# Late products in another order of units, the last quarter's in one PSUM bank, and a reordered program

## The chip, the cores and the metric

The kernel runs on one core of one Trainium2 chip. The metric is the time of one execution in microseconds (us). The core has five engines that work beside one another, each through its own queue of instructions: TensorE (PE in the rows; PEld is its loading of weights), VectorE (DVE), ScalarE (ACT), GpSimd (POOL) and SyncE (SP), which here only issues transfers. Rows with a "q" behind the engine are transfers that this engine issues; an engine's queue is worked off in order.

## The reference

One layer of a backbone over 1024 latent and 256 context tokens of width 1024: an S5 mixer (a scan over the tokens in both directions, with a complex diagonal matrix, in 64 groups of 16 channels and 64 states), GELU and a gated linear layer (GLU), then a SwiGLU feed-forward layer. Both are preceded by a norm with shift and scale and followed by a gate, all made from a conditioning vector.

```python
def run(u, h0):
    bu = jnp.einsum('lgh,gnh->lgn', u.astype(F32), b_bar)
    bu = bu.at[0].add(lam_bar * h0)
    a = jnp.broadcast_to(lam_bar, bu.shape)
    _, h = lax.associative_scan(_linear_combine, (a, bu), axis=0)
    return jnp.einsum('lgn,ghn->lgh', h, c_mat).real, h[-1]
...
def out(y, h):
    y = y.reshape(h.shape).astype(h.dtype) + d_skip * h
    g = jax.nn.gelu(y)
    return g * jax.nn.sigmoid(g @ w_glu + b_glu)
```

## The kernel before, in words

The 1024 latent tokens are cut into blocks of T = 8, so there are 128 of them and the scan only goes over the states at block ends. Within a block the output is a product with small Toeplitz matrices made from the powers of the diagonal; from the states it is a product with CL, which is C times powers. Everything is held for 64 groups, worked in four quarters q of 16 groups, or in eight k of 8 groups, or in sixteen units u of 4 groups (u = 2k, 2k + 1).

VectorE runs `scan()`: 32 steps of two blocks, then 63 single ones, one dependent on the next. States in between, which no later step needs, are filled in: those of q = 0 and q = 2 by VectorE itself, as extra operations put between the dependent ones (`one()`), those of q = 1 and q = 3 by GpSimd (`fill`).

Meanwhile the other engines work through a program, a string of letters with numbers that `run` turns into instructions in that order; each engine gets its own part of it:

- A n: conditioning products on TensorE up to tile n of 64 (`ada`, line 424), each from a 256 KB load on SyncE (line 417). The loads use a ring of eight buffers; the load of tile i + 8 is written down just ahead of product i.
- C q part: a fourth of CL of quarter q (`cl_gen`), two multiplications of 128x1024 by GpSimd and then their sum. HOW says by what: PE is two blocks of four products with the identity matrix on TensorE and copies on ScalarE, SY an adding DMA that GpSimd issues (line 549).
- K: Toeplitz values of a half quarter (`k_mats`): four products per round on TensorE (lines 619 to 627), a copy on ScalarE and a write to DRAM (kd) from ScalarE's queue. K0 and K1 belong to q = 0, K2 and K3 to q = 1, and so on.
- T u: reads unit u's matrix back from kd in Toeplitz form, on SyncE (`toeplitz`, line 639), into one of four buffers KQ, so T4 to T7 overwrite what the products of units 0 to 3 read.
- L, G: loads and signs C of a quarter; M: columns of the conditioning (`mod_cols`); B: copies of B; F: a fill on GpSimd.
- R k: "restacks" the states of k for the products, eight copies on ScalarE. P k: the products of the two units of k on TensorE (`inner_mm`, lines 745 and 750), which read KQ, the input U and the restacked states. Y u: copies unit u's sum from PSUM to Y on ScalarE.
- Z i: restacks the states of the other half of the block pairs (`late_restack`), on ScalarE, VectorE and GpSimd.

After the program comes the late loop, over i = 0 to 9, in the order `order = (6, 7, 4, 5, 0, 1, 2, 3)` of k: `late_mm` multiplies the late states with CL into PSUM (line 824); `late_add` adds that to Y on VectorE, a pair of operations per k; `late_act` takes GELU of Y on ScalarE; `gt_hi` and `gt_lo` transpose on TensorE (line 841) and split for the GLU. `restack` itself is lines 727 to 729. Two w_glu blocks and b_glu are loaded by SyncE ahead of the loop (lines 890, 893), into buffers that U and the conditioning held.

All waits are set by which buffer or PSUM bank an instruction reads or writes; the order on an engine is that of the program.

Of the kernel before, what the change touches and what calls it, by code (L numbers as in the profile page):

```python
# [37 lines left out]
def s5_ffn_kernel(tc, a, out):  # L38
# [3 lines left out]
    with ctx:  # L42
# [600 lines left out]
        def fill_ops(q, d, j):  # L643
            gs = slice(8 * q, 8 * q + 8)
            o = rot_ops(ST[:, 32 + 8 * j:39 + 8 * j:2, :, d, gs], ST[:, 31 + 8 * j:38 + 8 * j:2, :, d, gs], LQ[0],
                        32 * d + 8 * q, V, sf)
            return [o[0], o[2], o[1], o[3]]

        def scan():
# [14 lines left out]
            for k in range(32):  # L664
                step(LQ[1], 31 + 2 * k, 33 + 2 * k)
                if k % 4 == 3:
                    for d in range(2):
                        rest.extend(fill_ops(0, d, k // 4))
            for j in range(8):
                for d in range(2):  # L670
                    rest.extend(fill_ops(2, d, j))
# [5 lines left out]
        def fill(q, h, reg, kb):  # L677

            tmps = [view(reg, kb + i, [256]) for i in range(2)]
            gs, c0 = slice(8 * q, 8 * q + 8), 32 * h  # L680
            for d in range(2):
                rot(ST[:, 32 + c0:63 + c0:2, :, d, gs], ST[:, 31 + c0:62 + c0:2, :, d, gs], LS[:, 0], 32 * d + 8 * q, E, tmps)

        def mod_cols(part):
            r8 = view(RC[2], 0, [4, P])
# [52 lines left out]
        def inner_mm(k, hs):  # L738

            us = (2 * k, 2 * k + 1)  # L740
            for u in us:
                inner[u] = pw([4, T, HC])
# [3 lines left out]
            for u in us:  # L746
                for i in range(4):
                    for d in range(2):
                        cs_ = slice(64 * d, 64 * d + 64)
                        PE.matmul(flat(inner[u][cs_, i]), hs_of(hs, 4 * (u % 2) + i, cs_), flat(CL[u // 4][:, d, 4 * (u % 4) + i]),  # L750
                                  start=False, stop=i == 3)

        scan()
# [4 lines left out]
        HSl = [hstate(RXc, 0), hstate(RXc, 4), hstate(RA, 8), hstate(RA, 0)]  # L758
        order = (6, 7, 4, 5, 0, 1, 2, 3)
# [6 lines left out]
        def run(prog):  # L766


            for w in prog.split():
# [19 lines left out]
                elif op == "F":  # L789
                    fill(*divmod(i, 10), *((RA, 12) if i < 20 else (RXc, 4)))  # L790
# [6 lines left out]
                elif op == "P":  # L797
                    inner_mm(i, hse[i])
                elif op == "Y":
                    S.copy(yview(i), inner[i])  # L800

        HOW = ((PE,) * 4,) + ((SY,) * 4,) * 2 + ((SY, SY, PE, PE),)
        run("A24 A28 A32 C00 A36 C01 A40 A44 C02 A48 C03 K0 K1 L2 T0 T1 T2 T3 A52 A56 C10 C11 C12 C13 A60 A64 F10 F11 R0 P0 M0 M1 Y0 Y1"
            " G2 K2 K3 L3 R1 P1 T4 T5 T6 T7 Y2 Y3 B3 B2 M2 C20 C21 G3 R2 P2 R3 Y4 Y5 P3 Y6 Y7 C22 C23 K4 K5 T8 T9 T10 T11"
            " C30 C31 C32 R4 P4 Y8 Y9 C33 K6 K7 R5 P5 Y10 Y11 T12 T13 T14 T15 F30 F31 R6 P6 R7 Y12 Y13 P7 Z1 Z0 Y14 Y15")
# [9 lines left out]
        def late_mm(i):  # L815
            hs, ps_ = HSl[i % 4], []
            for n in range(2):
                u = 2 * order[i] + n
                po = pe8([4, T, HC])
                ps_.append(po)  # L820
                for j in range(4):
                    for d in range(2):
                        cs_ = slice(64 * (1 - d), 128 - 64 * d)
                        PE.matmul(flat(po[cs_, j]), hs_of(hs, 4 * n + j, cs_), flat(CL[u // 4][:, d, 4 * (u % 4) + j]),
                                  start=True, stop=True)
# [580 lines left out]
```

## Time and profile before

| | |
|---|---|
| median of three runs | 1128.93 us (1127.88 to 1129.6) |
| profiled execution, own time | 1129.6 us |
| its span | 1127.8 us |
| its mean granted TensorE clock | 0.952 |
| TensorE busy | 1003.2 us, 89% |
| VectorE busy | 819.8 us, 73% |
| GpSimd busy | 648.8 us, 58% |
| ScalarE busy | 415.9 us, 37% |

The span is one recorded execution, from its first to its last instruction; the own time of that execution is 1.8 us longer. The granted clock is a share of TensorE's full speed of 2.4 GHz; 0.50 is 1.2 GHz. The stretch that the change touches lies between some 130 us and 317 us; the GLU and the feed-forward layer follow. The rows that matter are shown further down.

### The profile page before, as it was taken

What the parts mean: (1) busy time and instruction counts of PE and PEld (TensorE: products, weight loads), DVE (VectorE), ACT (ScalarE), POOL (GpSimd) and SP (SyncE); (2) the same over time, 40 slices, a digit from 0 to 9 for tenths busy, and PEclk for the clock granted to TensorE, in tenths of its full rate; (3) what the DMA queues carried; (4) which work ended last, traced back from release to release, by engine and by line L of the source; (5) the groups of instructions that cost most, each with busy time, mean ns of one, the idle gap of its engine ahead of it and who ended that gap; (6) DMA issues with size and microseconds to landing.
All of it is one profiled execution on the core that took longest, in us unless ns stands there. A gap on an engine that the chain in (4) does not pass through costs nothing. (4 is left out here: it accounts for less than half of the span.)

```text
span 1127.8 us, 16572 instructions
## 1 busy us (share of the span) xinstructions
PE 1003.2 (89%) x6096; PEld 804.0 (71%) x6096; DVE 819.8 (73%) x1689; ACT 415.9 (37%) x873; POOL 648.8 (58%) x502
## 2 busy tenths in 40 slices
PE   4789791677978999889999999999999999999997
PEld 1268420455878997667888888888888888888875
DVE  8889899950667797998666666666666666666657
ACT  3378521425843455222222222222222222222236
POOL 4479968665274244866655555555555555555563
PEclk9699996878998999898999999999999999999999
DMA  9876778462422201101111111111111111111104
GB/s 351 316 157 122 221 242 196 111 135 65 125 87 76 76 1 58 56 19 57 56 42 36 38 55 57 57 57 56 56 56 57 56 57 56 57 56 56 48 29 149
DMA packets 51313, 103.12 MB, mean 91 GB/s; under 512 B 4256, under 2 KB 24992, under 8 KB 49184
## 3 DMA queue, kind: packets, MB, share of 16 engines
q1 hardware_dynamic: 43456, 85.67, 22.9%
q0 software_dynamic: 3456, 12.58, 6.1%
q10 hardware_dynamic: 4320, 3.81, 1.1%
q8 instruction: 48, 0.79, 0.3%
q14 instruction: 33, 0.27, 0.1%
HBM read 83.30 MB, written 6.16 MB: 79 GB/s over the span
## 5 line engine op out<-in xcount | busy, mean ns | idle before, releaser
L70 POOL TENSOR_TENSOR c<-rxc,c 128x512 fp32r<-128x512 f32 x128 | 169.8, 1342 | 186.4 <-ACT c L1060 183.1
L70 DVE TENSOR_TENSOR ru<-pd,ru 128x512 f32<-128x512 f32 x336 | 227.0, 690 | 2.4 <-PE pd L1116 2.3
L1116 PE MATMUL pu<-ra,c 128*128 128x512 f32 x432 | 168.6, 390 | 1.3 <-POOL c L70 1.2
L1115 PE MATMUL pu<-ra,c 128*128 128x512 f32 x432 | 168.2, 389 | 0.6 <-DVE ra L70 0.6
L1114 PE MATMUL pu<-ra,c 128*128 128x512 f32 x432 | 168.4, 390 | 0.3 <-ACT ra L1060 0.3
L1060 ACT CAST c<-rxc 128x512 fp32r<-128x512 f32 x128 | 76.7, 616 | 187.2 <-POOL rxc L70 107.2
L1114 PE MATMUL pd<-c 128*128 128x512 f32 x336 | 133.3, 397 | 10.9 <-DVE ru L70 10.9
L1115 PE MATMUL pd<-c 128*128 128x512 f32 x336 | 132.5, 394 | 0.0
L1116 PE MATMUL pd<-c 128*128 128x512 f32 x336 | 132.1, 393 | 0.0
L70 DVE TENSOR_TENSOR ru<-pu,ru 128x512 f32<-128x512 f32 x84 | 57.9, 689 | 87.1 <-PE pu L1116 52.9
L70 POOL TENSOR_TENSOR c<-ru,c 128x1024 fp32r<-128x1024 f32 x22 | 53.3, 2424 | 85.8 <-ACT c L858 77.1
L1116 PEld LDWEIGHTS pu<-ra,c 128*128 128x128 f32 x432 | 81.1, 188 | 19.7 <-POOL c L70 3.0
L1115 PEld LDWEIGHTS pu<-ra,c 128*128 128x128 f32 x432 | 81.1, 188 | 17.7 <-POOL c L70 0.9
L1114 PEld LDWEIGHTS pu<-ra,c 128*128 128x128 f32 x432 | 81.1, 188 | 17.6 <-ACT ra L1060 0.8
L1114 PEld LDWEIGHTS pd<-c 128*128 128x128 f32 x336 | 64.1, 191 | 26.2 <-DVE ru L70 12.9
L1116 PE MATMUL pu<-c,c 128*128 128x512 f32 x192 | 74.8, 390 | 0.3 <-POOL c L70 0.3
L1114 PE MATMUL pu<-c,c 128*128 128x512 f32 x192 | 74.9, 390 | 0.0
L1115 PE MATMUL pu<-c,c 128*128 128x512 f32 x192 | 74.7, 389 | 0.0
L1116 PEld LDWEIGHTS pd<-c 128*128 128x128 f32 x336 | 64.2, 191 | 13.6
L1115 PEld LDWEIGHTS pd<-c 128*128 128x128 f32 x336 | 64.2, 191 | 13.2
L70 POOL TENSOR_TENSOR c<-rxc,rxa 128x1024 f32<-128x1024 f32 x29 | 60.1, 2155 | 14.2 <-PE pw L546 10.6
L70 DVE TENSOR_TENSOR ru<-ru,rxa 128x512 f32<-128x512 f32 (+1 forms) x62 | 61.8, 998 | 7.5 <-ACT ru L1259 3.1
(292 smaller groups left out, 2227.3 us busy)
## 6 DMA issues: line engine op xcount, KB each, us to landing
c<-in_ada_w SPq DMA_DIRECT2D x48, 256.0 KB, 5.5
ru<-in_w SPq DMA_DIRECT2D x22, 512.0 KB, 3.6
c<-c POOLq DMA_DIRECT2D x19, 512.0 KB, 5.9
rxc<-in_w SPq DMA_DIRECT2D x38, 256.0 KB, 4.2
rxc<-in_w SPq DMA_DIRECT2D x19, 512.0 KB
ra<-in_ada_w SPq DMA_DIRECT2D x8, 1024.0 KB, 9.7
ru<-in_xT SPq DMA_DIRECT2D x4, 1024.0 KB, 6.2
ra<-in_ada_w SPq DMA_DIRECT2D x16, 256.0 KB, 6.4
```

The source lines that it names most:

```text
L70: eng.tensor_tensor(out=o, in0=x, in1=y, op=op)
L1060: S.copy(o[0], x)
L1114: PE.matmul(pu, wh, bh, start=start, stop=False)
L1115: PE.matmul(pu, wh, bl, start=False, stop=False)
L1116: PE.matmul(pu, wl, bh, start=False, stop=stop)
```

## The change

The late loop now goes over k in the order 4, 5, 6, 7, 0, 1, 2, 3. For k = 6 and 7 (`KP = 6`) the products of `inner_mm` are no longer issued in the program but inside `late_mm`, into a bank of the late loop's PSUM pool, and the late products accumulate in the same bank; GELU reads it from there, so Y12 to Y15 and the two `late_add` pairs of these k go. Their restacks R6 and R7 stay in the program, and the late states of i = 2 and 3 get other places (RA 24 and 28), since KQ and the restacked states are still in use.

VectorE now fills the states of the first half of q = 3 as well, and half of the columns of its second half: 176 extra operations instead of 128. GpSimd's F30 and F31 shrink to one F2, eight operations of 128x128. F10, F11 become F0, F1 with other temporaries.

C02, C03 and C32 are summed by adding DMAs instead of TensorE. The program's order changes throughout: C00 stands ahead of tile 24, 44 instead of 48 conditioning tiles stand ahead of K0; R0, R1 and G2 stand ahead of M0 and K2, P0 and P1 behind K3; P2 and P3 stand behind T7; R5 stands ahead of P4. The loads of wr0[1] and of b_glu go into the loop, at i = 3, and the order of the two splits of wr0 is turned round.

```diff
@@ -640,10 +640,10 @@
-        def fill_ops(q, d, j):
-            gs = slice(8 * q, 8 * q + 8)
-            o = rot_ops(ST[:, 32 + 8 * j:39 + 8 * j:2, :, d, gs], ST[:, 31 + 8 * j:38 + 8 * j:2, :, d, gs], LQ[0],
-                        32 * d + 8 * q, V, sf)
+        def fill_ops(e0, ne, d, c0, n):
+            es, c1 = slice(e0, e0 + ne), c0 + 2 * n - 1
+            o = rot_ops(ST[:, 32 + c0:32 + c1:2, :, d, es], ST[:, 31 + c0:31 + c1:2, :, d, es], LQ[0], 32 * d + e0, V, sf)
             return [o[0], o[2], o[1], o[3]]
         def scan():
@@ -665,24 +665,28 @@
                 step(LQ[1], 31 + 2 * k, 33 + 2 * k)
                 if k % 4 == 3:
                     for d in range(2):
-                        rest.extend(fill_ops(0, d, k // 4))
+                        rest.extend(fill_ops(0, 8, d, 2 * k - 6, 4))
             for j in range(8):
                 for d in range(2):
-                    rest.extend(fill_ops(2, d, j))
+                    rest.extend(fill_ops(16, 8, d, 8 * j, 4))
+            for e0, n in ((24, 4), (28, 2)):
+                for j in range(n):
+                    for d in range(2):
+                        rest.extend(fill_ops(e0, 4, d, 16 * j, 8))
             for k in range(64, 127):
                 step(LQ[0], 31 + k, 32 + k)
             while rest:
                 one()
-        def fill(q, h, reg, kb):
+        def fill(e0, ne, h, reg, kb):
             tmps = [view(reg, kb + i, [256]) for i in range(2)]
-            gs, c0 = slice(8 * q, 8 * q + 8), 32 * h
+            es, c0 = slice(e0, e0 + ne), 32 * h
             for d in range(2):
-                rot(ST[:, 32 + c0:63 + c0:2, :, d, gs], ST[:, 31 + c0:62 + c0:2, :, d, gs], LS[:, 0], 32 * d + 8 * q, E, tmps)
+                rot(ST[:, 32 + c0:63 + c0:2, :, d, es], ST[:, 31 + c0:62 + c0:2, :, d, es], LS[:, 0], 32 * d + e0, E, tmps)
         def mod_cols(part):
-            r8 = view(RC[2], 0, [4, P])
+            r8 = view(RC[2], 14, [4, P])
             if part == 0:
                 S.copy(r8, pm.rearrange("p (j n) -> p j n", j=4))
             elif part == 1:
@@ -735,11 +739,11 @@
             c0 = 64 * (u % 2)
             return Y[:, u // 2, :, c0:c0 + 64].rearrange("p t (g h) -> p g t h", g=4)
-        def inner_mm(k, hs):
+        def inner_mm(k, hs, pool):
             us = (2 * k, 2 * k + 1)
             for u in us:
-                inner[u] = pw([4, T, HC])
+                inner[u] = pool([4, T, HC])
                 for i in range(4):
                     kq = KQ[u % 4][:, i].rearrange("p (t h) -> p t h", t=T)[:, ::-1]
                     PE.matmul(inner[u][:, i], U[:, 4 * u + i, 32:160], kq, start=i == 0, stop=False)
@@ -748,15 +752,17 @@
                     for d in range(2):
                         cs_ = slice(64 * d, 64 * d + 64)
                         PE.matmul(flat(inner[u][cs_, i]), hs_of(hs, 4 * (u % 2) + i, cs_), flat(CL[u // 4][:, d, 4 * (u % 4) + i]),
-                                  start=False, stop=i == 3)
+                                  start=False, stop=i == 3 and k < KP)
+        KP = 6
         scan()
         inner, hse = {}, {}
         ct3 = [view(r, kb, [8, T, HC]) for r, kb in ((RU, 16), (RC[3], 12), (RXc, 4))]
         cts = [ct0 * 2, ct1 * 2, ct1 * 2, ct3 + ct3[2:]]
-        HSl = [hstate(RXc, 0), hstate(RXc, 4), hstate(RA, 8), hstate(RA, 0)]
-        order = (6, 7, 4, 5, 0, 1, 2, 3)
+        HSl = [hstate(RXc, 0), hstate(RXc, 4), hstate(RA, 24), hstate(RA, 28)]
+        order = (4, 5, 6, 7, 0, 1, 2, 3)
         def late_restack(i):
@@ -787,7 +793,7 @@
                     q, part = divmod(i, 10)
                     cl_gen(q, part, cts[q][part], HOW[q][part])
                 elif op == "F":
-                    fill(*divmod(i, 10), *((RA, 12) if i < 20 else (RXc, 4)))
+                    fill(*((8, 8, i, RC[3], 0) if i < 2 else (28, 4, 1, RU, 20)))
                 elif op == "T":
                     toeplitz(i)
                 elif op == "R":
@@ -795,14 +801,14 @@
                     for d in range(2):
                         restack(hse[i], 4 * i, d, 0, 64, (S, S, S, S))
                 elif op == "P":
-                    inner_mm(i, hse[i])
+                    inner_mm(i, hse[i], pw)
                 elif op == "Y":
                     S.copy(yview(i), inner[i])
-        HOW = ((PE,) * 4,) + ((SY,) * 4,) * 2 + ((SY, SY, PE, PE),)
-        run("A24 A28 A32 C00 A36 C01 A40 A44 C02 A48 C03 K0 K1 L2 T0 T1 T2 T3 A52 A56 C10 C11 C12 C13 A60 A64 F10 F11 R0 P0 M0 M1 Y0 Y1"
-            " G2 K2 K3 L3 R1 P1 T4 T5 T6 T7 Y2 Y3 B3 B2 M2 C20 C21 G3 R2 P2 R3 Y4 Y5 P3 Y6 Y7 C22 C23 K4 K5 T8 T9 T10 T11"
-            " C30 C31 C32 R4 P4 Y8 Y9 C33 K6 K7 R5 P5 Y10 Y11 T12 T13 T14 T15 F30 F31 R6 P6 R7 Y12 Y13 P7 Z1 Z0 Y14 Y15")
+        HOW = ((PE, PE, SY, SY),) + ((SY,) * 4,) * 2 + ((SY, SY, SY, PE),)
+        run("A22 C00 A24 C01 C02 C03 A44 K0 K1 L2 C10 C11 C12 C13 A52 T0 T1 T2 T3 F0 F1 A64 G2 B3 B2 R0 R1 M0 M1 K2 K3 L3 P0 P1"
+            " Y0 Y1 R2 T4 T5 T6 T7 Y2 Y3 R3 G3 C20 C21 M2 C22 C23 P2 P3 Y4 Y5 Y6 Y7 K4 K5 T8 T9 T10 T11 C30 C31 R4 R5 C32 P4 Y8 Y9 C33 F2"
+            " K6 K7 P5 Y10 Y11 T12 T13 T14 T15 R6 R7 Z0 Z1")
         psA.__exit__(None, None, None)
@@ -813,25 +819,32 @@
             return pE.tile([P] + list(shape), F32, tag=tag, name="pe", bufs=bufs)
         def late_mm(i):
-            hs, ps_ = HSl[i % 4], []
+            hs, k, ps_ = HSl[i % 4], order[i], []
+            new = k < KP
+            if not new:
+                inner_mm(k, hse[k], pe8)
             for n in range(2):
-                u = 2 * order[i] + n
-                po = pe8([4, T, HC])
+                u = 2 * k + n
+                po = pe8([4, T, HC]) if new else inner[u]
                 ps_.append(po)
                 for j in range(4):
                     for d in range(2):
                         cs_ = slice(64 * (1 - d), 128 - 64 * d)
                         PE.matmul(flat(po[cs_, j]), hs_of(hs, 4 * n + j, cs_), flat(CL[u // 4][:, d, 4 * (u % 4) + j]),
-                                  start=True, stop=True)
+                                  start=new, stop=new or j == 3)
             return ps_
         def late_add(i, ps_):
             k = order[i]
-            for n, po in enumerate(ps_):
+            for n, po in enumerate(ps_ if k < KP else ()):
                 tt(yview(2 * k + n), po, yview(2 * k + n), ADD)
-        def late_act(i):
-            S.activation(Y[:, order[i]], Y[:, order[i]], AF.Gelu_apprx_tanh)
+        def late_act(i, ps_):
+            if order[i] < KP:
+                S.activation(Y[:, order[i]], Y[:, order[i]], AF.Gelu_apprx_tanh)
+            else:
+                for n, po in enumerate(ps_):
+                    S.activation(yview(2 * order[i] + n), po, AF.Gelu_apprx_tanh)
         GH = [None, None]
@@ -886,11 +899,13 @@
         GHV = ()
         WSP, WSE, WSC, PRE = (5, 6), (E, E), (V, V), {8: (0,), 9: (1,)}
         wr0 = [view(RXa, 4, [1024]), view(RU, 36, [1024])]
-        for i in range(2):
+        bglu = view(RU, 32, [D])
+        def load_wr0(i):
             SY.dma_start(wr0[i].rearrange("p (k n) -> p k n", k=4),
                          a["w_glu"][512 * i:512 * i + 512, 0:256].rearrange("(k p) n -> p k n", p=P))
-        bglu = view(RU, 32, [D])
-        SY.dma_start(bglu, a["b_glu"].to_broadcast([P, D]))
+        load_wr0(0)
         ps_ = {}
         for i in range(10):
             if i < 8:
@@ -898,6 +913,8 @@
             if i + 2 < 8:
                 late_restack(i + 2)
             if i == 3:
+                load_wr0(1)
+                SY.dma_start(bglu, a["b_glu"].to_broadcast([P, D]))
                 HH = region("c3", 16, R32)
                 GH[0] = (view(HH, 0, [4, 8, P]), view(region("c2", 16, R32), 0, [4, 8, P]))
             if i >= 3:
@@ -907,12 +924,12 @@
             if i >= 3:
                 gt_lo(order[i - 3], 0, pt)
             if 1 <= i < 9:
-                late_act(i - 1)
+                late_act(i - 1, ps_[i - 1])
             if i == WSP[0]:
                 W0 = region("c0", 16, R32)
                 WR.append((view(W0, 0, [8 * 256]), view(W0, 8, [8 * 256])))
             if i in WSP:
-                j = 1 - WSP.index(i)
+                j = WSP.index(i)
                 v = slice(1024 * j, 1024 * j + 1024)
                 split(wr0[j], (WR[0][0][:, v], WR[0][1][:, v]), WSE[j], WSC[j])
             for s in PRE.get(i, ()):
```

SyncE's queue in the stretch of the first reload; `c_65` is the ring of conditioning tiles, the kd are the Toeplitz values of q = 0 to 3, "x" counts rows alike. A piece of the difference:

```order
-L417 DMA c_65<-in_ada_w 128x512 x39
+L417 DMA c_65<-in_ada_w 128x512 x43
 L639 DMA ra<-kd_1281 128x4x128 x4
-L417 DMA c_65<-in_ada_w 128x512 x9
+L417 DMA c_65<-in_ada_w 128x512 x5
```

Four loads move from behind T0 to T3 to ahead of them; the other reloads keep their place.

TensorE behind K1; `pm` are the conditioning sums, `pw` a PSUM bank of the program's, `kt` the Toeplitz values, and L745 and L750 (L749 and L754 after) are the products of a P:

```order
-L424 MATMUL pm<-c_65,r_60 2x512 x16
-L745 MATMUL pw<-ra,ru 128x128 x8
-L750 MATMUL pw<-c_63,ra 64x128 x16
-L691 MATMUL pw<-r_60,c_65 128x128 x4
+L424 MATMUL pm<-c_65,r_60 2x512 x20
+L695 MATMUL pw<-r_60,c_65 128x128 x4
 L619 MATMUL kt<-c_64,c_66 16x112 x4
```

Twenty conditioning products instead of sixteen stand here, and P0 has left the place ahead of K2.

TensorE from K7's last products to the fifth unit of the late loop, before; L745 and L750 are P5, P6 and P7, L824 the late products, L841 a transposition:

```order
L627 MATMUL kt<-rxc,rxa 16x16 x8
L745 MATMUL pw<-ra,ru 128x128 x8
L750 MATMUL pw<-c_65,ra 64x128 x16
L745 MATMUL pw<-ra,ru 128x128 x8
L750 MATMUL pw<-c_66,ra 64x128 x16
L745 MATMUL pw<-ra,ru 128x128 x8
L750 MATMUL pw<-c_66,ra 64x128 x16
L824 MATMUL pe<-c_66,rxc 64x128 x32
L824 MATMUL pe<-c_65,ra 64x128 x32
L841 MATMUL pe<-r_60,ru 128x128 x4
L824 MATMUL pe<-c_63,rxc 64x128 x16
```

And the same stretch after, where `pe` is a bank of the late loop's:

```order
L627 MATMUL kt<-rxc,rxa 16x16 x8
L749 MATMUL pw<-ra,ru 128x128 x8
L754 MATMUL pw<-c_65,ra 64x128 x16
L833 MATMUL pe<-c_65,rxc 64x128 x32
L749 MATMUL pe<-ra,ru 128x128 x8
L754 MATMUL pe<-c_66,ra 64x128 x16
L833 MATMUL pe<-c_66,ra 64x128 x16
L749 MATMUL pe<-ra,ru 128x128 x8
L754 MATMUL pe<-c_66,ra 64x128 x16
L833 MATMUL pe<-c_66,ra 64x128 x16
L854 MATMUL pe<-r_60,ru 128x128 x4
L833 MATMUL pe<-c_63,rxc 64x128 x16
```

The first late products, those of k = 4 and 5, now follow P5 at once, and P6 and P7 stand between them and the first transposition, each with its late part behind it.

## Rows read from the trace of the kernel before

**Rows 1.** Windows, the whole core: length, busy time and instructions per engine, granted clock, DMA.

```profile
460.00:1127.00 667.00, 647.11 (x2820) 531.70 (x2820) 457.50 (x638) 189.33 (x331) 375.45 (x271) 0.99 0.17 55
299.00:313.00 14.00, 11.62 (x144) 10.00 (x141) 13.68 (x24) 10.56 (x18) 4.74 (x2) 1.00 0.61 211
176.20:201.80 25.60, 6.52 (x19) 0.90 (x20) 25.60 (x147) 3.27 (x9) 16.55 (x20) 0.54 0.80 185
133.00:135.00 2.00, 0.10 (x4) 0.00 (x0) 1.93 (x6) 0.00 (x0) 1.92 (x4) 1.00 0.85 262
224.00:226.00 2.00, 0.35 (x1) 0.35 (x2) 1.86 (x9) 1.92 (x6) 2.00 (x2) 0.50 1.05 215
```

**Rows 2.** Timeline of VectorE; start, length, engine, line, operation, count, idle time before and releaser.

```profile
274.31 0.74 DVE L729 COPY rxc<-ra 64x256 f32<-64x256 f32 x2 [31.14 <-POOL ra L70]
295.87 1.29 DVE L70 TENSOR_TENSOR ru<-pe,ru 128x512 f32<-128x512 f32 x2
```

**Rows 3.** Timeline of TensorE, 130 to 210.

```profile
135.15 1.62 PE L424 MATMUL pm<-c,r 128*2 128x512 f32 x4 [2.06 <-DMA c<-in_ada_w]
...
161.68 1.02 PE L424 MATMUL pm<-c,r 128*2 128x512 f32 x2 [0.37 <-DMA c<-in_ada_w]
...
166.26 0.38 PE L619 MATMUL kt<-c,c 128*16 128x112 f32 x6
...
195.28 6.47 PE L424 MATMUL pm<-c,r 128*2 128x512 f32 x18 [22.02 <-DMA c<-in_ada_w]
...
206.15 0.39 PE L619 MATMUL kt<-c,c 128*16 128x112 f32 x8
```

**Rows 4.** Timeline of TensorE, 224 to 300.

```profile
225.65 2.08 PE L745 MATMUL pw<-ra,ru 128*128 128x128 f32 x8 [5.91 <-DMA ra<-kd]
...
236.36 1.13 PE L745 MATMUL pw<-ra,ru 128*128 128x128 f32 x8 [1.41 <-DMA ra<-kd]
...
239.32 0.39 PE L619 MATMUL kt<-c,rxa 128*16 128x112 f32 x8
...
264.41 0.38 PE L619 MATMUL kt<-c,rxa 128*16 128x112 f32 x6
...
269.51 2.05 PE L745 MATMUL pw<-ra,ru 128*128 128x128 f32 x16
...
278.74 4.19 PE L745 MATMUL pw<-ra,ru 128*128 128x128 f32 x16 [2.35 <-DMA ra<-kd]
...
285.82 2.05 PE L745 MATMUL pw<-ra,ru 128*128 128x128 f32 x16
...
289.61 3.66 PE L824 MATMUL pe<-c,rxc 128*64 128x128 f32 x64
...
297.28 1.97 PE L824 MATMUL pe<-c,rxc 128*64 128x128 f32 x32
```

**Rows 5.** Timeline of SyncE's issuing queue, five stretches of it.

```profile
176.17 6.81 SPq L639 DMA_DIRECT2D ra<-kd  x4
183.03 14.47 SPq L417 DMA_DIRECT2D c<-in_ada_w  x9
218.53 6.82 SPq L639 DMA_DIRECT2D ra<-kd  x4
247.74 4.37 SPq L639 DMA_DIRECT2D ra<-kd  x4
274.22 4.12 SPq L639 DMA_DIRECT2D ra<-kd  x4
```

**Rows 6.** All adding DMAs of GpSimd (line 549), issue to landing.

```profile
DMA to landing us min/median/max: 4.6/5.7/9.4
```

**Rows 7.** Timeline of GpSimd, two places.

```profile
134.59 10.05 POOL L70 TENSOR_TENSOR c<-rxc,rxa 128x1024 f32<-128x1024 f32 x5
...
237.63 2.03 POOL L70 TENSOR_TENSOR ru<-rxc,rxa 128x1024 f32<-128x1024 f32 x1 [4.12 <-PE pw L745]
```

**Rows 8.** Timeline of ScalarE, the restacks R6 and R7.

```profile
277.02 6.87 ACT L727 COPY ra<-ra 64x256 f32<-64x256 f32 x16
```

## The prediction

> **What bounds the kernel now.** I read the windows first, then the waits of VectorE, then the timeline of TensorE and of the issuing queues over the stretch that the diff touches. From 460 us to 1127 us TensorE is busy 647.11 of 667.00 us [rows 1]; the diff changes nothing there, so whatever is won or lost before the GLU moves the end by the same amount. Before that stands the scan on VectorE (it works in every moment of the window 176.20 to 201.80), and I looked for what follows its end: VectorE then does nothing for 31.14 us, until 274.31 [rows 2]. The scan is therefore not the bound of this stretch. What ends last is a chain through TensorE, ScalarE's small writes and SyncE's reloads: K matrices of a quarter on TensorE, Toeplitz tiles through DRAM (T), the products (P) that need them, then the next quarter. Its joints in the trace are K0 at 166.26, the last conditioning products at 195.28 after an idle 22.02 us, K2 at 206.15 [rows 3], K4 at 239.32, K6 at 264.41, and the late products from 289.61 [rows 4]. The idle 22.02 us is a queue: four T transfers are issued at 176.17 for 6.81 us, nine conditioning loads stand behind them on SyncE from 183.03 [rows 5], and the products K2 waits for come from the last of these loads.
>
> From 299 to 313 VectorE is busy 13.68 of 14.00 us and TensorE 11.62 [rows 1]: the end of the late loop is set by VectorE, which TensorE and ScalarE feed.
>
> **The change, hop by hop along that chain.** All times are those of the profiled execution (own time 1129.6, span 1127.8, so 1.8 lies around the span); it is 0.7 above the median of 1128.93.
>
> 1. K0. Two of the four quarter sums C00 to C03 leave TensorE (each a row block of 3.7 us with a wait for GpSimd ahead of it) for adding DMAs, and only 44 instead of 48 conditioning tiles precede K0. The tiles that were due between 135.15 and 161.68 are 24 [rows 3], about 1.1 us each, paced by their loads; four fewer are worth 4.4. Against it stand 1 MB more in DMAs in the same window, and C03's sum, whose landing K0 needs: the adding DMAs took 4.6 to 9.4 us, median 5.7 [rows 6]. GpSimd's five multiplications from 134.59 took 10.05 [rows 7], so its eight end near 152 to 154 when nothing holds them, and C03 lands 5.7 later, at 158 to 160. I take K0 at 161.5 instead of 166.26; bounds 158.5 (loads alone) and 164 (two slow DMAs).
>
> C00 now stands ahead of tile 24 and can't start before GpSimd has made it, two multiplications of 2.0 from 134.59, so TensorE is idle for 4 to 5 us before it. After 2.06 us of idle time at 133 to 135 the granted clock stayed at 1.00, which is 2.4 GHz; after 5.91 us of it, before 225.65, it was 0.50, 1.2 GHz [rows 1, 4]. The new gap lies between the two. The Trainium skill, "TensorE: Matmul & The Clock Gate", Part 1, says that idle time throttles the array again and that activity has to earn the speed back; the two rows agree that some idle times do and some don't. Were the clock to fall there, C00's block of eight would take 7.4 instead of 3.7 and K0 come near 163.5; if it stayed, near 160. The 161.5 above does not hang on it.
>
> 2. T0 stands behind 43 loads instead of 39, but the last of these need only tiles that TensorE takes right after K1, before the K matrices have landed. So T0 stays 9.9 behind K0 (176.17 less 166.26): 171.4.
>
> 3. The last conditioning product ended 25.6 after T0's issue: 201.75, by the row 195.28 + 6.47 [rows 3, 5]. Behind T now stand five loads, not nine, and the products run at half clock, 0.72 a tile (6.47 by nine): 2.9 less. Seven loads that had long landed are now just ahead of T, 1.8 MB at 185 to 257 GB/s, of which I let 1.3 us fall on T; bounds 0 and 5. So T0 + 24.0 = 195.4 (before 201.75).
>
> 4. K2. P0, a block of 4 us, no longer stands between. What is left is one copy on ScalarE and four small products, 1.5: K2 at 196.9 (before 206.15).
>
> 5. T4. K0 to T0 took 9.9, K2 to T4 12.4, with ScalarE late for K2 because of Y0, Y1 and G2, which the change puts elsewhere [rows 3, 5]. TensorE will be at half clock, as it was: I take 11.0, T4 at 207.9 (before 218.53). P0 and P1 now run between K3 and T6, and T6 and T7 overwrite what P1 reads; P1's Toeplitz part ends near 215, when SyncE would come to T7 anyway. Price if it doesn't: 1 to 3 us.
>
> 6. K4. It ended 20.8 after T4's issue, 17.8 of it the wait for the last T tile (236.36) [rows 4, 5]. Then three adding DMAs shared the queues, now two: 20.3, bounds 14 (the tiles land as T12 did, 4.5 after 274.22) and 22. K4 at 228.2 (before 239.32). R2, R3 and the fills F0, F1 for them are done before: GpSimd's queue ends them near 190 to 195, ScalarE's near 225.
>
> 7. K6. T8 is issued 8.4 after K4 (247.74); 6 to land (4.5 as after 274.22 is the fast end; 8.9, half of the 17.8 that four tiles took in hop 6, the slow one; two tiles are enough for P4, so I stay near the fast end) [rows 4, 5]; P4 after an idle stretch at half clock, 7.1 as P6 had from 278.74 to 285.82; C33's sum 3.7: 25, about what it was (25.1), without C32's block on TensorE and with P4 slower. The other arm, from C30's second product at 237.63 [rows 7] over C31 and C32 to C33, is 20 + 3.7, and not late. Bounds 22 and 29. K6 at 253.2 (before 264.41).
>
> 8. Late products. K7 ends 5.1 after K6 (269.51), P5 takes 3.8 (row 285.82 to 289.61), Y10, Y11 0.8 more, then ScalarE has R6 and R7, 6.87 for sixteen copies [rows 8], and three of Z0, 1.3. K6 + 17.9 = 271.1 (before 289.61). Only four of the twenty-five us from K6 to there fall away by order; P6 and P7 are gone from in front, and come back in the next hop.
>
> 9. Fifth unit. Before, the first two units of late products took 3.5 together (289.61 to the next pair), and the fifth, at 297.28, began 7.7 after the first. Now TensorE has been idle for some 8 us, so the first pair goes at half clock (6.8), then P6 and P7 stand here, each 3.9 with its late part of 1.9: 11.7, and one transposition 0.6. Together 19.1, bounds 15.5 (full clock) and 22. Fifth unit at 290.2 (before 297.28): 7.1 earlier. T12 to T15 land by K6 + 17 and P6 is not before K6 + 24.
>
> 10. Tail. In the VectorE-bound stretch one pair of additions (1.29 [rows 2]) falls away, because the accumulation is done in the bank; ScalarE loses four copies. 1.2 less.
>
> What I cost at nothing: 48 more state updates on VectorE. They are fitted between the dependent steps of the scan, where 147 instructions made 25.60 us in a window [rows 1], 0.17 each, a step of six in 1.05. Exposed entirely they add 48 x 0.17 = 8.4 and the scan ends near 251.6; its states are needed by R6 and Z0, after 262. Cover gone, 0 to 2.
>
> Sum: 7.1 + 1.2 = 8.3 earlier. Own time 1121.3; on the median 1120.6.
>
> **The rivals.**
>
> A larger gain. The second reload lands like the fourth (hop 6 with 14: 6.3 less) and the late pair and P4 go at full clock (3.3 each, of which I count half). For it: 4.5 us is measured at T12, and TensorE is busier ahead of K4. Against it: the window around T4 has adding DMAs and P1 to wait for. 8.3 + 6.3 + 3.3: about 1111.
>
> No change. The lead of 11 at K6 is spent in the late loop: P6 and P7 are 7.8 us of TensorE that stood under T12's wait and ScalarE's restacks, and now stand in the late chain. With hops 6 and 7 at their upper bounds (1.7 + 4) and hop 9 at 22 (2.9), 8.3 is gone: 1128 to 1130.
>
> Slower. The conditioning loads starve. C00 in front of tile 24 holds the ring of eight, so no load is issued while GpSimd makes C00; the later tiles come at 1.1 us each and K0 is at 170.0, 3.7 later than before; twenty tiles, not sixteen, are still behind K1, and T0 lies behind seven of their loads (hop 3 at its bound, 27.7). Then A ends at 207.6, K2 209.1, T4 220.1, K4 240.9, K6 265.9, late 283.8, fifth unit 302.9, less 1.2: 4.4 slower, 1133.3. It decides from about K0 at 166 with that bound. For it: the row at 161.68, where TensorE waited for a load just before K0. Against it: in the 26.5 us before, TensorE itself held the loads by waiting for GpSimd in front of C01 to C03.
>
> Not what it says. The order of units would free nothing if late products already waited on restacks alone; then only hop 10 stays, 1127.7. It falls under the second case.
>
> **Numbers.** Forecast and its neighbourhood (1115 to 1126) 0.60, larger gain 0.16, no change 0.12, slower 0.12. What a measurement can tell from no change is 0.2%, 2.3 us. Most of the no-change case lies within it (0.09), the rest on either side: faster 0.77, same 0.10, slower 0.13. The range, from the larger gain to just above no change, is 1110 to 1130; the hops' bounds in quadrature give 8 on either side.
>
> **What would show it.** Right: K0 near 161, conditioning products done by 196, K4 near 228, K6 near 253, the late products from 271 with P6 and P7 inside, the fifth unit near 290, VectorE's scan ending where it did. Wrong: K0 not before 166 (hop 1), T7 waiting on TensorE (hop 5), VectorE still scanning when R6 wants its states, or TensorE waiting between late units on ScalarE so that the fifth unit comes at 297 or later (hop 9).

## The result, and the profile after

The changed kernel is slower: 1131.57 us (median of 20 runs, 1127.36 to 1136.56) against 1129.28 (20 runs), a ratio of 1.003 with a 95% interval of 1.0017 to 1.0042. I had forecast 1120.6. Its profiled execution took 1130.35, with a span of 1128.5. The rival "slower" named the place that failed; its 1133.3 is 1.7 above the median, and for the profiled execution it would be 1129.6 + 4.4 = 1134.0, 3.7 too much.

Windows over the front (length, busy time per engine, clock, DMA share, GB/s). The changed kernel:

```profile
139.00:143.00 4.00, 4.00 (x5) 1.18 (x5) 3.86 (x8) 0.08 (x1) 4.00 (x3) 0.50 0.72 255
140.00:155.00 15.00, 11.93 (x36) 3.56 (x36) 14.52 (x47) 3.88 (x7) 14.40 (x10) 0.84 0.57 162
155.00:170.00 15.00, 10.57 (x31) 1.68 (x32) 15.00 (x87) 0.00 (x0) 11.16 (x7) 0.73 1.02 296
170.00:190.00 20.00, 12.54 (x188) 4.18 (x181) 20.00 (x116) 3.21 (x8) 17.91 (x21) 0.76 0.97 282
311.00:314.00 3.00, 3.00 (x17) 3.00 (x16) 0.28 (x1) 1.05 (x2) 0.00 (x0) 0.51 0.76 294
460.00:1127.00 667.00, 647.69 (x2824) 532.57 (x2822) 461.45 (x639) 190.26 (x332) 376.50 (x271) 0.99 0.17 55
```

The kernel before:

```profile
140.00:155.00 15.00, 14.79 (x44) 3.85 (x42) 14.62 (x64) 4.04 (x7) 9.71 (x6) 1.00 0.75 252
155.00:170.00 15.00, 13.17 (x142) 5.06 (x142) 15.00 (x86) 3.06 (x6) 9.36 (x6) 1.00 0.80 237
170.00:190.00 20.00, 2.72 (x82) 1.12 (x74) 20.00 (x115) 3.97 (x10) 18.87 (x20) 0.65 0.84 180
```

From 140 to 155 the changed kernel moves 162 GB/s where the old one moved 252; from 155 to 190 its DMA engines are full and catch up. The stretch from 460 on is the same, as forecast [rows 1]. TensorE, after (start, length, idle time before and its releaser in brackets), beside [rows 3, 4]:

```profile
133.09 1.88 PE L424 MATMUL pm<-c,r 128*2 128x512 f32 x12
138.50 6.46 PE L546 MATMUL pw<-c,r 128*128 128x512 f32 x8 [3.52 <-POOL c L70]
144.90 1.03 PE L424 MATMUL pm<-c,r 128*2 128x512 f32 x4
...
150.13 1.90 PE L424 MATMUL pm<-c,r 128*2 128x512 f32 x16
154.72 3.30 PE L424 MATMUL pm<-c,r 128*2 128x512 f32 x6 [2.69 <-DMA c<-in_ada_w]
158.75 2.34 PE L424 MATMUL pm<-c,r 128*2 128x512 f32 x6 [0.72 <-DMA c<-in_ada_w]
163.37 2.32 PE L424 MATMUL pm<-c,r 128*2 128x512 f32 x4 [2.28 <-DMA c<-in_ada_w]
167.12 3.04 PE L424 MATMUL pm<-c,r 128*2 128x512 f32 x6 [1.43 <-DMA c<-in_ada_w]
169.25 0.35 PE L619 MATMUL kt<-c,c 128*16 128x112 f32 x1
...
201.59 4.12 PE L424 MATMUL pm<-c,r 128*2 128x512 f32 x10 [10.39 <-DMA c<-in_ada_w]
...
206.98 0.39 PE L619 MATMUL kt<-c,c 128*16 128x112 f32 x8
...
233.64 0.38 PE L619 MATMUL kt<-c,rxa 128*16 128x112 f32 x8
...
251.90 3.75 PE L749 MATMUL pw<-ra,ru 128*128 128x128 f32 x16 [13.77 <-DMA ra<-kd]
...
261.52 0.38 PE L619 MATMUL kt<-c,rxa 128*16 128x112 f32 x6
...
278.36 0.69 PE L833 MATMUL pe<-c,rxc 128*64 128x128 f32 x2 [7.77 <-ACT rxc L731]
279.23 5.91 PE L833 MATMUL pe<-c,rxc 128*64 128x128 f32 x62 [0.19 <-ACT rxc L731]
...
296.92 1.97 PE L833 MATMUL pe<-c,rxc 128*64 128x128 f32 x32
```

SyncE's queue after, beside [rows 5]:

```profile
176.33 7.55 SPq L417 DMA_DIRECT2D c<-in_ada_w  x7
188.27 4.06 SPq L639 DMA_DIRECT2D ra<-kd  x4
192.44 3.90 SPq L417 DMA_DIRECT2D c<-in_ada_w  x5
216.79 4.82 SPq L639 DMA_DIRECT2D ra<-kd  x4
```

To be read from these rows: TensorE waits 3.52 for C00, then four times for loads (7.12 in all); K0 is at 169.25; T0 is issued 19.0 behind it (before: 9.9); the last loads' products wait 10.39.

How many loads SyncE issues while this happens, in the stretch from 137 to 151, first in the changed kernel and then before:

```profile
145.95 0.80 SPq L417 DMA_DIRECT2D c<-in_ada_w  x2
```

```profile
143.28 7.23 SPq L417 DMA_DIRECT2D c<-in_ada_w  x12
```

The changed stretch doesn't begin at the same moment in each execution: the first product from the ring lies between 128.2 and 136.6 in fourteen profiles of kernels that are alike up to there. So I compare distances along the chain, in us, each from one profiled execution. "First product" is the first product of the ring, that is, the first conditioning product whose tile comes from the ring of eight; "late" and "fifth" are the first and the fifth unit of late products:

| kernel | first product to K0 | K0 to T0 | K0 to last cond. product | K2 to K4 | K4 to K6 | K6 to late | late to fifth | fifth to end |
|---|---|---|---|---|---|---|---|---|
| before | 35.1 | 9.9 | 35.5 | 33.2 | 25.1 | 25.2 | 7.7 | 830.5 |
| forecast | 30.3 | 9.9 | 33.9 | 31.3 | 25.0 | 17.9 | 19.1 | 829.3 |
| after | 36.2 | 19.0 | 36.5 | 26.7 | 27.9 | 16.8 | 18.6 | 831.6 |
| after, again | 36.8 | 20.2 | 37.5 | 25.3 | 27.8 | 16.8 | 18.2 | 831.6 |
| old front | 34.9 | 9.9 | 35.1 | 25.8 | 26.3 | 16.8 | 17.5 | 831.1 |
| old order, new sums | 31.1 | 14.3 | 36.3 | 28.2 | 28.6 | 16.8 | 18.4 | 831.2 |
| reload first | 36.4 | 11.3 | 32.6 | 26.0 | 29.5 | 16.8 | 18.8 | 831.4 |
| products before | 35.9 | 20.5 | 38.7 | 30.5 | 28.7 | 23.6 | 7.7 | 832.5 |
| C00 behind tile 32 | 28.4 | 17.8 | 40.0 | 31.1 | 28.0 | 16.8 | 18.6 | 832.1 |
| loads first only | 36.2 | 22.1 | 27.3 | 30.3 | 28.2 | 18.4 | 17.5 | 830.6 |
| loads before reload | 32.3 | 22.2 | 26.0 | 27.8 | 28.7 | 16.8 | 18.5 | 831.5 |
| late states first | 36.3 | 19.5 | 35.9 | 26.2 | 28.5 | 10.2 | 18.4 | 831.5 |
| both orders | 30.7 | 23.7 | 28.2 | 34.4 | 25.9 | 10.2 | 18.4 | 831.4 |
| both, old split | 31.7 | 22.7 | 27.0 | 27.8 | 28.5 | 10.2 | 18.4 | 828.7 |
| old split | 36.6 | 20.2 | 38.8 | 26.4 | 28.2 | 16.9 | 18.5 | 829.0 |

From the ring's first product to the end, the two profiles of the changed kernel take 995.4 and 995.3, the one of before 996.6. So the profiles don't show the 2.3 us by which the median of the changed kernel is above that of before; where these come from stays open. What the profiles show is where the 8.3 us of the forecast went.

### The profile page after: what moved, and what is told of

It reads as the page before. It is cut to its first block, busy times and chain, and to the rows that moved or that the text cites. A ratio compares the mean times of both kernels' runs of the same rounds, so it can differ in the third digit from the quotient of the medians.

```text
span 1128.5 us, 16551 instructions
## 1 busy us (share of the span) xinstructions
PE 993.0 (88%) x6072; PEld 800.6 (71%) x6072; DVE 823.5 (73%) x1733; ACT 410.5 (36%) x865; POOL 640.6 (57%) x497
## 4 chain that ended last, share of the span: by engine, by line
PE 65%; DVE 18%; ACT 6%; DMA 3%; issue 2%; POOL 1%; SPq 0%; ACTq 0%; DVEq 0%; POOLq 0%
PE pu L1133 11%; PE pu L1132 11%; PE pu L1131 10%; PE pd L1131 6%; PE pd L1132 6%; PE pd L1133 6%; DVE ru L70 6%; DVE ra L70 3%; DVE rxa L70 3%; PE pw L473 2%; PE pe L893 2%; PE pe L892 2%; PE pe L894 2%; DVE c L70 1%; DVE ltb L70 1%
## 5 line engine op out<-in xcount | busy, mean ns | idle before, releaser
L70 POOL TENSOR_TENSOR c<-rxc,c 128x512 fp32r<-128x512 f32 x128 | 169.3, 1338 | 185.3 <-ACT c L1077 179.0
L1131 PE MATMUL pd<-c 128*128 128x512 f32 x336 | 133.3, 397 | 10.9 <-DVE ru L70 10.9
L1131 PEld LDWEIGHTS pu<-ra,c 128*128 128x128 f32 x432 | 81.1, 188 | 17.5 <-ACT ra L1077 0.8
L1131 PEld LDWEIGHTS pd<-c 128*128 128x128 f32 x336 | 64.4, 192 | 26.3 <-DVE ru L70 12.9
L70 DVE TENSOR_TENSOR ru<-ru,rxa 128x512 f32<-128x512 f32 (+1 forms) x62 | 64.5, 1040 | 6.9 <-ACT ru L1276 2.9
```

The source lines that it names most:

```text
L70: eng.tensor_tensor(out=o, in0=x, in1=y, op=op)
L1131: PE.matmul(pu, wh, bh, start=start, stop=False)
```

## The experiments

Ratios are to the kernel before, run on the same chip, with 95% intervals.

**The old front.** Front of the program and C00 to C03's sums as before:

```diff
-HOW = ((PE, PE, SY, SY),) + ...
+HOW = ((PE,) * 4,) + ...
-A22 C00 A24 C01 C02 C03 A44 K0 K1 L2 C10 C11 C12 C13 A52 T0 T1 T2 T3 F0 F1 A64 G2 ...
+A24 A28 A32 C00 A36 C01 A40 A44 C02 A48 C03 K0 K1 L2 T0 T1 T2 T3 A52 A56 C10 C11 C12 C13 A60 F0 F1 A64 G2 ...
```

> The changed kernel with the first part of the old program and the old sums of C00 to C03 (all on TensorE), P0 and P1 still behind K3 and everything from K2 on as in the changed kernel. Theory A (the front half starves: C00 in front of tile 24 holds the load ring, the loads are then caught up with while the adding DMAs and the kd writes want the same queues): K0 back at 166 (changed: 169.3), T0 at 176 (188.3), last conditioning product at 201 or sooner (205.7), fifth late unit at 291 to 293 (296.9), time 1126 to 1128, 4 us under the changed kernel. Rival B (the front's losses are absorbed anyway by a later wait, on GpSimd's C20 to C23 or on the reload T8): K0 as before, but the late products within 1 us of the changed kernel's 278.4 and the time within 1.5 us of it.

Measured: 1127.73 (0.9982, 0.9956 to 1.0008). K0 at 166.6, T0 9.9 behind it, last conditioning product at 201.7, late products at 271.9, fifth unit at 289.4 in an execution of 1122.25. Theory A holds in the trace, rival B falls. The profiled execution was one of the fastest of its twelve runs, so its 7 us against the kernel before must not be read as the gain; the median is some 4 us under the changed kernel's, with overlapping intervals against that kernel's second measurement (further down). This run changes the place of C00 and the kind of sum together; the next ones part them.

**The old order with the new sums**: the front as just shown, HOW as in the changed kernel.

> As the run with the old front, but C02 and C03 are summed by adding DMAs as in the changed kernel. If the place of C00 (the held ring) is the cause, this is like the old front: K0 at 163 to 166, T0 9.9 to 11 behind it, the time within 1 us of that run. If the 1 MB of adding DMAs itself is the cause, K0 is at 168 or later with its wait on the sum's landing, T0 over 14 behind K0, and the time is that of the changed kernel, 1130 to 1132.

Measured: 1124.96 (0.9949, 0.9928 to 0.9971). K0's first product comes 31.1 behind the ring's first product, four less than with the old sums, as hop 1 had it. But K0's later products need C02 and C03, and they wait for the adding DMAs:

```profile
168.13 0.28 PE L619 MATMUL kt<-c,c 128*16 128x112 f32 x2 [1.56 <-DMA c<-c]
```

So the first kd write goes out 35.0 behind the ring's first product (36.9 in the old front): half of the gain is gone. ScalarE's fourth copy then waits 3.67 for an earlier kd write to land, where in the old front it waits for none, and T0, 45.4 behind the ring's first product, is no earlier than there (44.8). Each of the two cases of the expectation is right in part: K0's first product is as early as in the first, the wait for the sums and T0's 14.3 behind K0 are those of the second. The time is not that of the changed kernel, and the interval lies under both of its intervals; the equality with the old front within 1 us is neither shown nor excluded (2.8 apart, intervals overlap).

**The reload first**: `T0 T1 T2 T3` moved ahead of `C10 C11 C12 C13 A52`. C10 to C13 issue nothing on SyncE, so in its queue T0 to T3 change places with seven loads.

> The changed kernel with T0 to T3 written ahead of tiles 45 to 52, so that they stand behind 36 conditioning loads on SyncE instead of 43. Theory A: the queues are full either way; K0 stays at 169, T0 comes when the kd writes land, at 183 to 188, the twelve loads behind it land later, the last conditioning product at 206 to 210, time 0 to 4 us slower than the changed kernel. Rival C (only the seven loads just ahead of T0 delay it): T0 at 180, last conditioning product at 203, time 2 us faster than the changed kernel.

Measured: 1129.74 (0.9987, 0.9965 to 1.0009). T0 comes 11.3 behind K0 instead of 19.0, so seven loads just ahead of it made 7.7 of its delay. The last conditioning product is 32.6 behind K0 instead of 36.5. Rival C is right on what delays T0; its 2 us are what the medians show, but the intervals overlap.

**C00 behind tile 32**:

```diff
-A22 C00 A24 C01 C02 C03 A44 K0 ...
+A32 C00 C01 C02 C03 A44 K0 ...
```

> The changed kernel with C00 to C03 behind tile 32 and not behind tile 22; the sums by adding DMA, the order of T0 to T3 behind 43 loads and all else stay. Theory A (the held ring): TensorE's waits for loads before K0 (7.1 us in the changed kernel) are under 3 us, K0 at 163 to 167 (169.3), last conditioning product 2 to 5 us sooner, time 2 to 5 us under the changed kernel. Rival B (the adding DMAs crowd the loads wherever C00 stands): K0 at 168 or later, time within 1 us.

Measured: 1126.98 (0.9987, 0.9967 to 1.0006). K0's first product is at 160.4, 28.4 behind the ring's first product; my 161.5 would have been 30.3. K0's later products, though, wait here too for the adding DMAs of C02 and C03, and the last conditioning products for their loads:

```profile
163.99 0.37 PE L619 MATMUL kt<-c,c 128*16 128x112 f32 x2 [1.84 <-DMA c<-c]
...
195.95 4.43 PE L424 MATMUL pm<-c,r 128*2 128x512 f32 x10 [8.17 <-DMA c<-in_ada_w]
```

So the place of C00 to C03 is worth 7.8 us at K0's first product and 5.5 at the first kd write (33.6 behind the ring's first product, 39.1 in the changed kernel). Of the 7.8, idle time of TensorE is 4.9 (11.0 in the changed kernel, 6.15 here), and 3.3 is the time that the products of C00 and C01 take: 10.42, partly at half clock, against 7.13 at full clock. The waits for loads are 6.15 and not under 3, as theory A had them; 3.55 of it lies behind the sums, where the changed kernel has 7.12.

T0 is 9.0 us earlier, counted so, but of that only 4.2 are left at the last conditioning product (68.4 behind the ring's first product, after 72.6): T0 to T3, which still stand ahead of the last five loads, take 10.20 to issue instead of 4.06. The ratio is 0.3 to 0.4% under the two of the changed kernel; against the second the intervals overlap.

**The products before**: KP = 8, so P6, P7 and Y12 to Y15 go back into the program.

```diff
-T12 T13 T14 T15 R6 R7 Z0 Z1
+T12 T13 T14 T15 R6 P6 R7 Y12 Y13 P7 Z0 Z1 Y14 Y15
```

> The changed kernel with P6, P7 and their copies Y12 to Y15 back in the program ahead of Z0, and four late additions more on VectorE (KP = 8); the order of units 4 to 7, 0 to 3 stays. My forecast of hops 8 to 10 (the products inside the late loop cost as much there as they free ahead of it, less one pair of additions): fifth unit 0 to 3 us later than the changed kernel's 296.9, time 0 to 3 us slower. Rival (P6 and P7 inside the loop keep ScalarE and VectorE idle while TensorE works, and the tail then loses its clock): fifth unit later but the end the same or earlier, time 0 to 2 us faster.

Measured: 1129.12 (0.9999, 0.9972 to 1.0026), 2.7 us under the changed kernel's 1131.85, with overlapping intervals. From K6 to the end 863.8 in its profile, 867.0 in the changed kernel's, 863.4 before. The profiled execution, 1137.58, was the slowest of its twelve, so only its distances are used. My expectation has the wrong sign in them: as ordered, the late half costs 3 us. The rival's story (an earlier end by a warmer tail) isn't it either; the tail is 832.5. The next run shows where the time is lost: in the wait of 7.77 ahead of the late products and in the first pair at half clock (0.69 and 5.91).

**Late states first**: Z0 and Z1 ahead of R6 and R7.

```diff
-R6 R7 Z0 Z1
+Z0 Z1 R6 R7
```

> The changed kernel with Z0 and Z1 ahead of R6 and R7 on ScalarE (6.64 us of copies for R6 and R7 stood ahead of Z0 and TensorE waited 7.77 us for it). Theory D (the late half of the change loses what the front gives because the first late products wait on ScalarE behind R6 and R7, with a cold clock afterwards): first late products 11 to 13 after K6 instead of 16.8, fifth unit 28 to 31 after K6 instead of 35.4, time 4 to 6 us under the changed kernel. Rival E (P6 waits for R6 or for T12 anyway): first late products as early as that, but P6 late, fifth unit 33 or more after K6, time within 2 us of the changed kernel.

Measured: 1124.73 (0.9963, 0.9946 to 0.998). The late products come 10.2 behind K6, the fifth unit 28.5, and from K6 to the end it is 860.0 instead of 867.0. TensorE in this run:

```profile
273.05 0.43 PE L833 MATMUL pe<-c,rxc 128*64 128x128 f32 x2 [1.12 <-ACT rxc L731]
273.90 3.71 PE L833 MATMUL pe<-c,rxc 128*64 128x128 f32 x62 [0.42 <-ACT rxc L731]
```

The wait is 1.12, and the pair's main part takes 3.71 and not 5.91. Theory D holds; the median is 7.1 us under the changed kernel's 1131.85, and the intervals don't overlap.

**The loads before the reload**, on the run with the old order and the new sums:

```diff
-L2 T0 T1 T2 T3 A52 A56 C10 C11 C12 C13 A60 F0 F1 A64 G2
+L2 A52 A56 C10 C11 C12 C13 A60 A64 T0 T1 T2 T3 F0 F1 G2
```

> The run with the old order and the new sums, but T0 to T3 now stand behind all conditioning loads on SyncE. Theory A2 (the chain goes through the last conditioning load, since K2 and C20's buffer wait for its product; T0 to T3 are wanted only by P0): last conditioning product at 188 to 192 (201.8 in that run), C20 on GpSimd at 194 to 197 behind the fills (205), K4 at 222 to 226 (231.2), time 5 to 8 us under that run, 1117 to 1120. Rival B2 (the queues are full, so the order of the same bytes doesn't matter, and P0 to P3 become late instead): last conditioning product at 195 or later or K4 within 2 us, time within 2 us of 1125.

Measured: 1124.1 (0.9961, 0.9936 to 0.9986). Last conditioning product at 190.7, K4 at 224.7, as A2 had them. Counted from the ring's first product, the last conditioning product comes 9.1 earlier than in the run with the old order and the new sums (58.3 for 67.4), but K2 only 4.1: TensorE now waits there for a copy on ScalarE that stands behind the restacks of R0 and R1:

```profile
195.89 1.11 PE L695 MATMUL pw<-r,c 128*128 128x128 f32 x4 [5.23 <-ACT c L691]
```

At K4 4.5 are left (92.3 for 96.9). The profiled run took 1122.02 against that run's 1128.04, 2.0 of it because it reached the first product sooner. The medians, 1124.1 and 1124.96, don't part, and A2's time of 1117 to 1120 was missed: that the gain at K4 reaches the median of this pair isn't shown.

**The loads first only**, the same edit on the changed kernel (`A52 T0 T1 T2 T3 F0 F1 A64 G2` becomes `A52 A64 T0 T1 T2 T3 F0 F1 G2`):

> The changed kernel with T0 to T3 behind all conditioning loads on SyncE, C00 still behind tile 22. Theory A2 (the chain goes through the last load): last conditioning product 8 to 12 us sooner than the changed kernel's 36.5 after K0, so 24 to 28 after K0, time 3 to 7 us under the changed kernel. Rival B2 (the held ring has set the loads back for good): 30 or more after K0, time within 2 us.

Measured: 1125.31 (0.9958, 0.9935 to 0.9981), against 1.0016 (0.9992 to 1.0041) of the changed kernel beside it: 6.5 faster by the medians, with intervals that don't overlap. The last conditioning product is 27.3 behind K0 (36.5), and K2 66.1 behind the ring's first product (73.9). From the ring's first product to the end it is 991.1 instead of 995.4, so the profile shows 4.3 of it. Its SyncE queue:

```profile
160.43 26.01 SPq L417 DMA_DIRECT2D c<-in_ada_w  x18
186.54 26.15 SPq L639 DMA_DIRECT2D ra<-kd  x8
```

T0 is 22.1 behind K0, 2 to 3 us more than without the edit (19.0 and 20.2), and the five loads no longer wait for it. Theory A2 holds, B2 falls.

**The changed kernel again:**

> The changed kernel itself once more, beside the others. All theories: 0.2 to 0.4% over the kernel before, and in the profile K0 at 169 to 173, the last conditioning product at 204 to 211, the fifth unit at 296 to 303.

Measured: 1131.85, K0 36.8 behind the ring's first product, fifth unit at 294.5. Its distances are those of the first profile within 1.4.

**The old split**: `j = 1 - WSP.index(i)` in place of `j = WSP.index(i)`.

> The changed kernel with only the order of the two splits put back. Theory F: 1 to 3 us faster than the changed kernel, GpSimd's first operation of the GLU 0.5 to 2.5 us sooner against the fifth unit (21.9 us behind it in the changed kernel, 20.3 before). Rival G: the same within 0.5 us.

Measured: 1130.17 (1.0002, 0.9976 to 1.0027), 1.7 under the changed kernel, within both intervals. In the profile the tail is 829.0 instead of 831.6. TensorE in the changed kernel, then in the run with both orders and the old split:

```profile
307.75 0.38 PE L892 MATMUL pe<-c,c 128*128 128x256 f32 x1 [0.22 <-DVE c L873]
310.19 0.39 PE L893 MATMUL pe<-c,c 128*128 128x256 f32 x1 [2.06 <-POOL c L70]
...
311.78 0.41 PE L894 MATMUL pe<-c,c 128*128 128x256 f32 x1
...
312.63 1.06 PE L854 MATMUL pe<-r,ru 128*128 128x128 f32 x4
```

```profile
295.05 0.39 PE L893 MATMUL pe<-c,c 128*128 128x256 f32 x1 [1.14 <-POOL c L70]
```

And the window behind that wait in the same run:

```profile
296.00:299.00 3.00, 3.00 (x28) 3.00 (x28) 0.93 (x3) 1.67 (x3) 0.00 (x0) 1.00 0.73 288
```

The GLU's first products go over k = 4 to 7 and then 0; the turned order split the half for k = 0 to 3 first. So in the changed kernel TensorE waited 2.06 behind the very first product for the second split, and the granted clock from 311 to 314 was 0.51. With the old order only the last of these five k waits, 1.14, and the clock is 1.00.

**Both orders** (old order, new sums, loads before the reload, late states first), and **the same with the old split**:

> The two orders together: the run with all loads ahead of the reload, and Z0 and Z1 ahead of R6 and R7. If both theories (A2 and D) hold, the gains add: 9 to 14 us under the run with the old order and the new sums (1125), 1111 to 1116. If only one holds, 1117 to 1121. If neither, 1124 to 1126.

> The run with both orders, and the two splits of wr0 in the old order (second half first). The first products of the GLU need the second half of wr0 (k = 4 to 7) and only their last three the first half. Theory F (the turned split order makes TensorE wait 2.06 us for GpSimd's second split, the clock then falls to 0.50 for 3 us, and the transpositions of the last units are late): that wait is under 1.2 us, the clock stays at 1.00, from the last GELU to the end 814 to 815 us instead of 816.6, time 1 to 3 us under the run with both orders. Rival G (the tail is set by GELU and GpSimd's later work): the wait goes, the end moves less than 0.5 us.

Measured: 1115.25 (0.9873, 0.9833 to 0.9912, six runs) and 1111.99 (0.9837, 0.9804 to 0.987, six runs). The second beats both kernels by 18 to 20 us. The first is 9.7 under the run with the old order and the new sums, as expected if the gains add; in its profile 7.1 of that show from the ring's first product to the end (984.8 for 991.9), with the last conditioning product 28.2 behind K0 and the late products 10.2 behind K6, so both orders do their part. Theory F's 2.7 in the tail is in the profile, 3.3 by the medians with overlapping intervals.

## Why the prediction was wrong

By the profiled execution the forecast of 1121.3 was 9.05 too low. Along the table's columns (after less forecast, with A for the last conditioning product): +5.9 at K0, +2.6 from K0 to A, -0.2 from A to K2, -4.6 from K2 to K4, +2.9 to K6, -1.1, -0.5, +2.3 in the tail, and +1.9 because this execution reached the first product at 133.1 and not 131.2, which isn't of the change. The sum is 9.2.

- Hop 1 failed, and it is the largest term: "K0 at 161.5" took the pace of the loads as given and forgot who issues them. From 135.0, while TensorE waited for C00 and worked on it, no product of the ring ran until 144.9, so no buffer came free. The loads on their way landed and little followed: SyncE issued two loads from 137 to 151, where before it issued twelve. TensorE paid behind C01, with 7.12 of waits for loads. The run with C00 behind tile 32 shows that the place is the cause: K0's first product comes 7.8 earlier there, the first kd write 5.5. The slower rival said just this, with K0 at 170.0, the last product at 207.6 and K2 at 209.1; after had 169.3, 205.7 and 207.0. I gave it 0.12, because TensorE had held the loads before, too. What I left out is that before, eight products ran between 135 and C00, and freed buffers for the loads that SyncE issued from 143.3 on.
- The clock sentence in hop 1: after 3.52 of idle time the granted clock was 0.50 from 139 to 143 and C00's block took 6.46, not 3.7. The rule of the Trainium skill that stands there ("TensorE: Matmul & The Clock Gate", Part 1) agrees with this trace. The half clock held TensorE, and with it the ring, the longer; the prediction said that its 161.5 did not hang on it, but the 2.8 us are part of the 5.9.
- The wait for C03's sum, which hop 1 did have, does not show in the changed kernel, where the loads come later still. It shows with 1.56 and 1.84 in two runs that bring K0 forward.
- Hop 2 failed by 9: T0 came 19.0 behind K0. The seven loads, written off as "landed", were issued until 183.9, and the run with the reload first gives 7.7 of it back. Hop 3 failed the other way by 6.6: from T0 to the last conditioning product it took 17.4 and not 24.0, the five loads behind T3 having been issued in 3.90, where before nine took 14.47 [rows 5]. That only +2.6 is left at A is two errors that cancel, so luck.
- Hops 4 and 5 held in size (A to K2 1.3 for 1.5; K2 to T4 9.8 for 11.0). Hop 6 was too careful: K4 came 16.9 behind T4's issue, not 20.3. In the old front's trace the last of C20 to C23 is issued at 221.7 and K4 comes at 228.7, so this arm, which starts at A, is not far behind; I had not counted it, and no run tries it apart.
- Hop 7: 27.9 for 25. T8 was issued 10.9 behind K4 (244.6), not 8.4; ScalarE's fourth copy waited 3.2 for an earlier kd write to land, with adding DMAs in flight. What part these have wasn't tried apart.
- Hops 8 and 9 held (16.8 and 18.6 for 17.9 and 19.1), and their reason was right: ScalarE's restacks and half clock. I took the order of R and Z as unavoidable; putting Z ahead of R6 and R7 takes 6.6 us from hop 8.
- Hop 10 had the wrong sign: -1.2 forecast, +1.1 measured. The pair of additions did go, and GELU ended 14.8 behind the fifth unit instead of 16.2. But the turned split order, for which the prediction has no price, gave it back: with the old split order the tail is 829.0, 1.5 less than before.
- The 48 state updates cost nothing that shows: the scan ended at 247.1 (before: 243.2), and R6, which needs its states, came at 271.2.

Why the slower rival's total was still too large: its K4 of 240.9 was 7.3 late, since hop 6 went well (it had put 20.8 there). And that its 1133.3 is so near the median is in part luck, since along the chain of the profile the changed kernel is not slower than before.

Not tried apart are the order of the units, which the change begins with, and the fills that moved from GpSimd to VectorE.

## What to carry to other kernels

A wait put in front of a consumer that frees a ring is a wait for the loads behind the ring, too: count the buffers that come free while it lasts, and don't carry the pace of loads over from another point. Before a queue's order is changed, ask which of its transfers the chain waits for next, and put the others behind; what is won there can still be lost at the next wait, as K2's wait for ScalarE shows. When the order of consumers is turned, check that the order of their producers is turned the same way.

## What the runs showed of the hardware

An idle time of 3.52 us ahead of C00 was followed by half clock (a block of 6.46 that takes 3.70 before). So was the 2.06 us at 310, while the 2.06 us at 133 to 135 of before was not [rows 1, 3]. So the length of an idle time alone doesn't tell; what does, no run here tries apart.

From 155 to 190, with the DMA engines at a share of 1.02 and 0.97, the four adding DMAs of 512 KB took 6.9 to 8.3 us to land; before, at 0.80 and 0.84, four took 4.6 to 9.4. The medians are 7.2 and 6.2, so a difference is not shown.
